# A two-layer fp32 encoder on one core: later casts of the turned attention weights, a new order of the output projections and end, and 16-bit DMA transposes for the residual and for rotated queries and keys

## The chip, the cores and the metric

The kernel runs on 1 core of one Trainium2 chip. The metric is the device time of one execution in microseconds; the kernel before was timed in 3 runs. Engines are named as in the profile: PE (TensorE matmul) and PEld (its weight load), DVE (VectorE), ACT (ScalarE), POOL (GpSimd), SP (SyncE, which issues almost all DMAs).

## The reference

An encoder trunk over 256 tokens of width 2048, all in float32: one even layer, one odd layer, a final RMSNorm.

```python
h = x
y = rms_norm(h, norm_g[0]); h = h + even_layer(y, w_in_even[0], w_out_even[0], rpb_b[0])
y = rms_norm(h, norm_g[1]); h = h + odd_layer(y, w_in_odd[0], w_out_odd[0], sinks_c[0], qnorm_d[0], knorm_d[0])
return rms_norm(h, final_g)
```

Each layer has 16 heads of 128 in two branches of 8 heads. Even: a dilated window attention with a distance penalty, and a two-dimensional neighbourhood attention with a learned bias. Odd: a windowed attention with a sink logit (branch C), and a dense attention with normalised and rotated queries and keys (branch D); four query heads share a key and value head. Each branch's output is multiplied by a SiLU gate; the gated outputs are concatenated and go through the output projection (2048 x 2048), whose result is added to h.

## The kernel before, in words

**The weight stream.** All projections are one stream of 272 weight tiles of 128 x 1024 floats, in the order of a list (`plan`). For each tile, called a weight step below and counted from 0: SP loads `wraw` (five buffers), ACT casts it to the rounded high part `whi` (L70), DVE subtracts to get the low part `wlo` (L71), both with three buffers, and PE runs its matmuls: high times high, high times low, low times high. The weights of a step are cast two steps ahead. In-projections of the even layer are steps 0 to 127, its output projection 128 to 159, in-projections of the odd layer 160 to 239, its output projection 240 to 271.

**Everything else runs beside it.** After each weight step, `step()` (L224) advances three queues of generators by one `yield`: `evac` (results out of PSUM), `post` (rotation of queries and keys), `bg` (attention, advanced twice if two are queued). What an engine does in which order follows from the order in which the program issues it and from a scheduler; DMAs issued with `pinned` (L86) keep their place in program order.

**Attention.** `attend` (L387) handles a pair of heads, in stages separated by yields: logits of both heads on PE, `probs` (exponentials on ACT, normalising at L430 or L432), `turned` and `joined`, `weigh` (the product with the values on PE). The probabilities must be transposed between `probs` and `weigh`. That is done in 16-bit halves: POOL takes the words apart (`ph`, L440), SP issues two DMA transposes (`pa`, L88), POOL joins the words again (`pt`, L451), ACT casts the high part (`pth`, L93), DVE subtracts for the low part (`ptl`, L94). `joined` issues the last three together, two yields after `turned`. Pairs 0 to 3 and 4 to 7 are the two branches of a layer; in the odd layer branch D (4 to 7) comes first.

**Rotation.** `normed_rope` (L329) scales queries or keys of branch D, rotates them on DVE into `ru`, and three yields later transposes them on PE (four 128 x 128 transposes, L353) into PSUM, from where ACT (L96) and DVE (L97) split them. It runs five times: one key pair, four query pairs.

**Output projection.** `close_layer` (L604) goes through the four column blocks of 512 (n) with all pairs but the last, then drains the attention queues, and then does the last pair's product for all four blocks in the tail. In the even layer the tail (L616) also makes the next layer's input: for each block, 8 transposes of h on PE (L626), splits into `x` by ACT and DVE, and the squares for the norm. In the odd layer the last pair's four weight tiles are brought in ahead, into the room of `x`, and `tail_odd` (L716) ends the kernel: for each half of the tokens (t) the last products, the squares, the reciprocal root by three Newton steps on DVE (L164), and the scaling of h and its way out in eight DMAs.

## Time and profile before

| | |
|---|---|
| time, median of 3 runs | 839.02 us (837.39 to 839.69) |
| profiled execution: its own time | 838.58 us |
| its span | 836.8 us, mean TensorE clock 0.993 |
| TensorE busy | 97% of the span |
| VectorE, ScalarE, GpSimd busy | 69%, 53%, 13% |
| chain that ended last | PE 72%, DMA 8%, DVE 7%, issue 4%, POOL 3%, ACT 3%, SPq 2% |
| read from HBM | 155.64 MB, 190 GB/s over the span |

The profile is of one execution. A row of the timeline gives start, duration, engine, line, operation, what it writes and reads, and in brackets how long the engine had been idle and what it waited for. Matmuls are pipelined, so the distance between their starts counts, not their duration. PEclk is the clock granted to TensorE as a share of full speed.

### The profile page before, as it was taken

Reading aid. Unit: us, or ns where it says so; the run is one execution under the profiler, and the core shown is the slowest. Engines: PE = TensorE matmul, PEld = TensorE weight load, DVE = VectorE, ACT = ScalarE, POOL = GpSimd, SP = SyncE. Lnnn points to the kernel's source line nnn. Section 1 sums busy time; section 2 is a strip of 40 time slices with the busy share of each in tenths; the row PEclk is TensorE's granted clock in tenths of the full one; section 3 lists DMA queues with packets and bytes.
Section 4 is the critical chain, followed back from the end, with each engine's and each line's share of the span. In section 5 each row is a group of like instructions: output and inputs, shape, how many; then the busy total and the mean of one; then the engine's idle time right before and its main releaser. Section 6 shows DMA issues by size and latency. Waiting matters only on the chain.

```text
span 836.8 us, 11845 instructions
## 1 busy us (share of the span) xinstructions
PE 813.5 (97%) x4344; PEld 695.9 (83%) x4344; DVE 576.5 (69%) x873; ACT 443.1 (53%) x706; POOL 108.6 (13%) x88
## 2 busy tenths in 40 slices
PE   7999999999999999999999999999999999998995
PEld 5888888888888888888888888888798888876884
DVE  5676775677756786687645877877966776675547
ACT  6755554554545554555443745667456655564433
POOL 0002020022203040040100000012222123211000
PEclk9999999999999999999999999999999999999998
DMA  8966775675755766675755555555676677867622
GB/s 276 375 221 210 264 189 202 210 212 156 223 200 153 248 179 217 199 193 186 213 184 194 168 185 185 192 168 173 176 185 195 201 237 196 210 198 207 209 88 100
DMA packets 90394, 166.91 MB, mean 199 GB/s; under 512 B 48928, under 2 KB 49824, under 8 KB 90272
## 3 DMA queue, kind: packets, MB, share of 16 engines
q1 hardware_dynamic: 90192, 166.14, 64.0%
q8 instruction: 34, 0.56, 0.3%
q14 instruction: 24, 0.20, 0.1%
q10 hardware_dynamic: 144, 0.02, 0.0%
HBM read 155.64 MB, written 3.05 MB: 190 GB/s over the span
## 4 chain that ended last, share of the span: by engine, by line
PE 72%; DMA 8%; DVE 7%; issue 4%; POOL 3%; ACT 3%; SPq 2%; POOLq 0%; DVEq 0%; ACTq 0%
PE ps_f L251 24%; PE ps_f L255 12%; PE ps_t L104 11%; PE ps_t L103 10%; PE ps_t L105 10%; DMA pa<-ph 4%; DVE wlo L71 3%; DMA wraw<-in_even_t 2%; SPq L88 2%; POOL ph L440 2%; POOL pt L451 2%; ACT whi L70 1%; DMA h<-in_x 1%; PE ps_out L104 1%; PE ps_out L105 1%
## 5 line engine op out<-in xcount | busy, mean ns | idle before, releaser
L71 DVE TENSOR_TENSOR wlo<-wraw,whi 128x1024 fp32r<-128x1024 f32 (+1 forms) x269 | 340.1, 1269 | 151.4 <-ACT whi L70 149.7
L70 ACT CAST whi<-wraw 128x1024 fp32r<-128x1024 f32 (+1 forms) x269 | 279.9, 1046 | 230.2 <-PE ps_t L105 120.6
L251 PE MATMUL ps_f<-x,whi 128*128 128x512 f32 x1184 | 373.0, 396 | 0.0
L255 PEld LDWEIGHTS ps_f<-x,wlo 128*128 128x128 f32 x1184 | 222.5, 189 | 58.0 <-DVE wlo L71 6.0
L255 PE MATMUL ps_f<-x,wlo 128*128 128x256 f32 x1184 | 234.3, 279 | 3.2 <-DVE wlo L71 3.0
L251 PEld LDWEIGHTS ps_f<-x,whi 128*128 128x128 f32 x1184 | 181.3, 189 | 0.4
L103 PE MATMUL ps_t<-whi,x 128*128 128x512 f32 (+1 forms) x256 | 98.0, 383 | 4.7 <-ACT x L96 4.7
L440 POOL COPY ph<-pr 128x1024 uint16<-128x1024 uint16 x32 | 40.3, 1261 | 443.9 <-ACT pr L430 264.1
L104 PE MATMUL ps_t<-wlo,x 128*128 128x512 f32 (+1 forms) x256 | 97.4, 381 | 0.3 <-DVE wlo L71 0.3
L104 PE MATMUL ps_t<-wlo,mh 128*128 128x512 f32 x240 | 95.1, 396 | 2.1 <-DVE wlo L71 2.1
L105 PE MATMUL ps_t<-whi,x 128*128 128x512 f32 (+1 forms) x256 | 97.1, 379 | 0.0
L103 PE MATMUL ps_t<-whi,mh 128*128 128x512 f32 x240 | 94.5, 394 | 2.0 <-ACT whi L70 2.0
L105 PE MATMUL ps_t<-whi,ml 128*128 128x512 f32 x240 | 94.1, 392 | 0.0
L93 ACT CAST pth<-pt 128x512 fp32r<-128x512 f32 x32 | 19.8, 620 | 84.9 <-POOL pt L451 84.9
L451 POOL COPY pt<-pa 128x1024 uint16<-128x1024 uint16 x32 | 54.2, 1693 | 45.3 <-DMA pa<-ph 45.3
L103 PEld LDWEIGHTS ps_t<-whi,x 128*128 128x128 f32 x256 | 48.7, 190 | 13.5 <-ACT x L96 5.3
L94 DVE TENSOR_TENSOR ptl<-pt,pth 128x512 fp32r<-128x512 f32 x32 | 22.1, 689 | 53.8 <-ACT pth L93 53.8
L105 PEld LDWEIGHTS ps_t<-whi,x 128*128 128x128 f32 x256 | 48.6, 190 | 9.1
L104 PEld LDWEIGHTS ps_t<-wlo,x 128*128 128x128 f32 x256 | 48.8, 191 | 8.9 <-DVE wlo L71 0.7
L104 PEld LDWEIGHTS ps_t<-wlo,mh 128*128 128x128 f32 x240 | 45.5, 190 | 12.4 <-DVE wlo L71 3.6
L103 PEld LDWEIGHTS ps_t<-whi,mh 128*128 128x128 f32 x240 | 45.5, 189 | 11.7 <-ACT whi L70 2.5
L105 PEld LDWEIGHTS ps_t<-whi,ml 128*128 128x128 f32 x240 | 45.5, 190 | 9.3
(116 smaller groups left out, 665.0 us busy)
## 6 DMA issues: line engine op xcount, KB each, us to landing
wraw<-in_even_f SPq DMA_DIRECT2D x96, 512.0 KB, 3.9
wraw<-in_odd_f SPq DMA_DIRECT2D x56, 512.0 KB, 4.0
wraw<-in_w_out_even SPq DMA_DIRECT2D x32, 512.0 KB, 3.3
wraw<-in_w_out_odd SPq DMA_DIRECT2D x32, 512.0 KB, 4.0
wraw<-in_even_t SPq DMA_DIRECT2D x31, 512.0 KB, 4.5
wraw<-in_odd_t SPq DMA_DIRECT2D x24, 512.0 KB, 3.3
h<-in_x SPq DMA_DIRECT2D x4, 512.0 KB, 8.1
bias<-in_bias_a SPq DMA_DIRECT2D x8, 256.0 KB, 5.5
```

What stands on the lines that cost most here:

```text
L70: nc.scalar.copy(self.hi[:, c], raw[:, c])
L71: nc.vector.tensor_sub(self.lo[:, c], raw[:, c], self.hi[:, c].bitcast(F32))
L88: tc.keep_in_program_order(nc.sync.dma_start(dst, src, **kw))
L93: nc.scalar.copy(hi, src)
L94: nc.vector.tensor_sub(lo, src, hi.bitcast(F32))
L103: nc.tensor.matmul(dst, lh, rh, start=first, stop=False, skip_group_check=True)
L104: nc.tensor.matmul(dst, lh, rl, start=False, stop=False, skip_group_check=True)
L105: nc.tensor.matmul(dst, ll, rh, start=False, stop=last, skip_group_check=True)
L251: nc.tensor.matmul(acc[:, f, :], w.hi[:, c], xx[k], start=k == 0, stop=False, skip_group_check=True)
L255: nc.tensor.matmul(acc[:, f, :S], w.lo[:, c], xh[k], start=False, stop=k == KC - 1, skip_group_check=True)
L440: nc.gpsimd.tensor_copy(halves, words)
L451: nc.gpsimd.tensor_copy(words.bitcast(U16).rearrange("p c (q s) -> p s c q", s=2), st[i])
```

## The change

- **Turning in two functions.** `turn` (POOL's halves, SP's two transposes) and `join` (POOL's words) are taken out of the attention, to be used in three places.
- **Attention.** `joined` comes one yield after the second `turned` instead of two; the cast of `pth` and the subtraction of `ptl` are a stage of their own, `parted`, a yield later. ACT's cast keeps its place in program order.
- **Queues.** `step()` advances `post` twice if two are queued. `need(pr)` advances the queues until a pair is done.
- **Rotation.** The four PE transposes become a turn: a yield, `turn`, two yields, `join`, a yield, then the split of the words, ACT's part of it in program order.
- **Residual.** For each finished column block `next_input` turns h in two parts (8 turns in all) and splits the words into `x`, where 32 PE transposes stood.
- **Output projection.** Two column blocks are accumulated side by side: six pairs of block 0, six of block 1, then pair 7 and pair 8 of the order for both; then blocks 2 and 3 one after the other with all eight pairs. Nothing waits for a drain before the last pair. In the odd layer the last four pairs of block 3 are kept for the end, their weights in the room of `x`; the squares of blocks 0 to 2 are taken as each is finished, and they are multiplied by the final gain ahead of the end.
- **End.** For each half of the tokens, the last four products of block 3, the square, and the reciprocal root as Sqrt on ACT, reciprocal and one Newton step on DVE; for the second half of the tokens the last product, its sum and square come in two parts of 256 columns. The output leaves in ten DMAs.

```diff
         for queue in (evac, post, bg):
             advance(queue)
+        if len(post) > 1:
+            advance(post)
...
+    def turn(tag, tag2, src, bufs):
+        halves = tp.tile([P, 2, 2, S], U16, tag=tag, name="halves", bufs=bufs)
+        across = tp.tile([P, 2, 2, S], U16, tag=tag2, name="across", bufs=bufs)
+        nc.gpsimd.tensor_copy(halves, src.bitcast(U16).rearrange("p t (k s) -> p t s k", s=2))
+        for t in range(2):
+            pinned(
+                across[:, :, :, t * P : (t + 1) * P].rearrange("p s c q -> p (s c) q"),
+                halves[:, t].rearrange("p s k -> p (s k)"), transpose=True,
+            )
+        return across
+
+    def join(tag, across, bufs):
+        words = tp.tile([P, 2, S], F32, tag=tag, name="words", bufs=bufs)
+        nc.gpsimd.tensor_copy(words.bitcast(U16).rearrange("p c (q s) -> p s c q", s=2), across)
+        return words
...
         nc.vector.tensor_add(u, u, w)
-        for _ in range(3):
-            yield
-        tr = ps_at.tile([P, 2, S], F32, tag="at", name="ps_tr")
-        for t in range(2):
-            for hh in range(2):
-                nc.tensor.transpose(tr[:, hh, t * P : (t + 1) * P], u[:, t, hh, :], ident)
+        yield
+        across = turn("tmp2", "tmp2", u.rearrange("p t h d -> p t (h d)"), 2)
+        yield
+        yield
+        words = join("tmp2", across, 2)
+        yield
         dst = pair(tag)
-        split(*dst, tr, scale)
+        tc.keep_in_program_order(nc.scalar.mul(dst[0], words, scale))
+        nc.vector.scalar_tensor_tensor(
+            out=dst[1], in0=words, scalar=scale, in1=dst[0].bitcast(F32), op0=ALU.mult, op1=ALU.subtract
+        )
...
+        def parted(i):
             hi = tp.tile([P, 2, S], F32R, tag="pth", name="pth")
             lo = tp.tile([P, 2, S], F32R, tag="ptl", name="ptl")
-            split(hi, lo, words)
+            tc.keep_in_program_order(nc.scalar.copy(hi, st[i]))
+            nc.vector.tensor_sub(lo, st[i], hi.bitcast(F32))
...
         turned(1)
         yield
-        yield
         joined(0)
         yield
         joined(1)
+        parted(0)
+        yield
+        parted(1)
         yield
...
+    def out_order(kind):
+        order = ORDER[kind]
+        seq = [(n, pr) for n in range(2) for pr in order[:6]]
+        seq += [(n, pr) for pr in order[6:] for n in range(2)] + [(2, pr) for pr in order]
+        return seq + [(3, pr) for pr in (order if kind == "even" else order[:4])]
...
-            for c in range(2):
-                tr = ps_at.tile([P, 2, S], F32, tag="at", name="ps_ht")
-                for i in range(2):
-                    for t in range(2):
-                        nc.tensor.transpose(
-                            tr[:, i, t * P : (t + 1) * P],
-                            h[n][:, t, (2 * c + i) * P : (2 * c + i + 1) * P], ident,
-                        )
+    def next_input(n):
+        across = [turn("lg", "pr", h[n][:, :, c * S : (c + 1) * S], 2) for c in range(2)]
+        for c in range(2):
+            words = join("lg", across[c], 2)
+            for i in range(2):
+                k = 4 * n + 2 * c + i
+                split(xh[k], xl[k], words[:, i, :], gcol[:, KC + k : KC + k + 1])
+        square_sums(parts1, n)
...
+    def scale_of(ss, rest):
+        root, y, x, half, u, r = [col(name) for name in ("root", "y", "x", "half", "u", "r")]
+        pin(nc.scalar.activation(root, ss, AF.Sqrt, bias=rest, scale=1.0 / D))
+        pin(nc.vector.tensor_scalar(x, ss, 1.0 / D, rest, ALU.mult, ALU.add))
+        pin(nc.vector.tensor_scalar_mul(half, x, -0.5))
+        pin(nc.vector.reciprocal(y, root))
+        pin(nc.vector.tensor_scalar(u, y, y, half, ALU.mult, ALU.mult))
+        pin(nc.vector.tensor_scalar(r, u, 1.5, y, ALU.add, ALU.mult))
+        return r
...
+    for j, pr in enumerate(late[:3]):
+        product_out(accs[1], final[j], pr, 1, False, False)
+    ss = []
+    for c in halves:
+        product_out(accs[1], final[3], late[3], 1, False, True, c)
+        ss.append(added(1, c))
+    rest = col("rest")
+    pin(nc.vector.tensor_scalar(rest, ss[0], 1.0 / D, sums[:, 1:2], ALU.mult, ALU.add))
+    r = scale_of(ss[1], rest)
+    finish(0, 1, r, halves[0])
+    finish(0, 1, r, halves[1])
+    finish(1, 1, r, scalar=True)
+    finish(3, 1, r, halves[0])
+    finish(3, 1, r, halves[1])
+    finish(2, 1, r)
```

What an engine has in its queue is compared at three places. First ACT at the last attention of branch C, where the output projection of the odd layer begins. In a row stand line, operation, what it writes and reads (numbers are tiles), and the shape; `pr` are the probabilities, L430 and, in the change, L443 normalise them. Before:

```order
L422 ACTIVATE pr_7389,den_7390<-lg_7336,mn_7335 128x257 x2
L70 CAST whi_7367<-wraw_7366 128x1024
L430 ACTIVATE pr_7389<-pr_7389,rden_7393 128x256 x2
L70 CAST whi_7398<-wraw_7397 128x1024
L93 CAST pth_7466<-pt_7464 128x512
L70 CAST whi_7429<-wraw_7428 128x1024
L93 CAST pth_7490<-pt_7488 128x512
```

And of the change the same stretch of ACT:

```order
L435 ACTIVATE pr_7400,den_7401<-lg_7347,mn_7346 128x257 x2
L443 ACTIVATE pr_7400<-pr_7400,rden_7404 128x256 x2
L70 CAST whi_7378<-wraw_7377 128x1024
L70 CAST whi_7410<-wraw_7409 128x1024
L70 CAST whi_7433<-wraw_7432 128x1024
L70 CAST whi_7453<-wraw_7452 128x1024
L457 CAST pth_7472<-words_7450 128x512
L70 CAST whi_7477<-wraw_7476 128x1024
L457 CAST pth_7494<-words_7470 128x512
```

Between the second head's normalising and the first `pth` there is one weight cast before, and four in the change.

Second, ACT in the output projection of the even layer, where column block 0 becomes the odd layer's input `x0`. Before, with `ps_ht` the PSUM tile that PE's transposes wrote:

```order
L185 ACTIVATE junk_4435,parts_3794<-h0_91 128x512
L185 ACTIVATE junk_4437,parts_3794<-h0_91 128x512
L96 ACTIVATE x0_87<-ps_ht_4417,gcol_95 128x256
L96 ACTIVATE x0_87<-ps_ht_4426,gcol_95 128x256
L96 ACTIVATE x0_87<-ps_ht_4417,gcol_95 128x256
L70 CAST whi_4484<-wraw_4483 128x1024
L96 ACTIVATE x0_87<-ps_ht_4426,gcol_95 128x256
```

And in the change, where `words` is POOL's joined tile and `whi_4246` and `whi_4264` are the weights of steps 147 and 148:

```order
L168 ACTIVATE junk_4176,parts_3794<-h0_91 128x512
L168 ACTIVATE junk_4178,parts_3794<-h0_91 128x512
L70 CAST whi_4228<-wraw_4227 128x1024
L168 ACTIVATE junk_4222,parts_3794<-h1_92 128x512
L168 ACTIVATE junk_4224,parts_3794<-h1_92 128x512
L70 CAST whi_4246<-wraw_4245 128x1024
L96 ACTIVATE x0_87<-words_4164,gcol_95 128x256 x2
L96 ACTIVATE x0_87<-words_4170,gcol_95 128x256 x2
L70 CAST whi_4264<-wraw_4263 128x1024
L70 CAST whi_4282<-wraw_4281 128x1024
L96 ACTIVATE x1_88<-words_4210,gcol_95 128x256 x2
```

The splits read POOL's tile instead of PE's, and stand two weight casts behind the block's squares, in front of the weight of step 148; the last product of block 0 is step 142.

Third, ACT at the first attention of branch D (probabilities `pr_5342` before). Before:

```order
L96 ACTIVATE qh_5284<-ps_tr_5279 128x512
L70 CAST whi_5316<-wraw_5315 128x1024
L422 ACTIVATE pr_5342,den_5343<-ps_s_5306,mn_5313 128x256 x2
L430 ACTIVATE pr_5342<-pr_5342,rden_5346 128x256 x2
L70 CAST whi_5351<-wraw_5350 128x1024
L422 ACTIVATE pr_5373,den_5374<-ps_s_5333,mn_5340 128x256 x2
L430 ACTIVATE pr_5373<-pr_5373,rden_5377 128x256 x2
L70 CAST whi_5387<-wraw_5386 128x1024
L93 CAST pth_5406<-pt_5404 128x512
```

And in the change, where `qh_5227` is the second pair of queries and `pr_5298` the first head's probabilities:

```order
L70 CAST whi_5307<-wraw_5306 128x1024
L304 ACTIVATE ge_5285<-qf_5281 128x512
L365 ACTIVATE qh_5227<-words_5203 128x512
L443 ACTIVATE pr_5298<-pr_5298,rden_5302 128x256 x2
L70 CAST whi_5343<-wraw_5342 128x1024
L435 ACTIVATE pr_5329,den_5330<-ps_s_5289,mn_5296 128x256 x2
L443 ACTIVATE pr_5329<-pr_5329,rden_5333 128x256 x2
L70 CAST whi_5369<-wraw_5368 128x1024
L457 CAST pth_5364<-words_5360 128x512
L70 CAST whi_5398<-wraw_5397 128x1024
```

The cast of the second queries now reads POOL's `words` and stands directly in front of the first head's normalising, where before it read PSUM and stood a weight cast ahead of the exponentials.

More of the change, by code (lines that the diff above doesn't have):

```diff
@@ L757, in encoder, with beside @@
-    close_layer(ORDER["odd"], tail_odd, ahead)
+    gfin, final = [], []
+    parts2 = sm.tile([P, 2, NN], F32, tag="parts", name="parts")
+    late = ORDER["odd"][4:]
+    def beside(n, i):
+        if (n, i) == (2, 0):
+            for m in range(NN):
+                gfin.append(pp.tile([P, 512], F32, tag="bias", name="gfin", bufs=4))
+                nc.sync.dma_start(gfin[m], a["final_g"][m * 512 : (m + 1) * 512].partition_broadcast(P))
+        if n == 2 and i % 2:
+            j = i // 2
+            room = X[j].rearrange("p k c t -> p (k c t)")
+            final.append(Weights(a["w_out_odd"][NN - 1][late[j]], room[:, :1024], room[:, 1024:]))
+        if (n, i) in ((2, 4), (2, 6), (3, 1)):
+            m = i // 2 - 2 if n == 2 else 2
+            for t in range(2):
+                nc.vector.tensor_mul(h[m][:, t, :], h[m][:, t, :], gfin[m])
@@ new lines, in encoder @@
+    accs = project_out("odd", lambda n: square_sums(parts2, n), beside)[NN - 1]
+    pin = tc.keep_in_program_order
+    full, halves = slice(0, 512), [slice(0, 256), slice(256, 512)]
+    sums = sm.tile([P, 2], F32, tag="sums", name="sums", bufs=1)
+    nc.vector.tensor_reduce(sums, parts2[:, :, : NN - 1], AX.X, ALU.add)
+    nc.vector.tensor_scalar(sums, sums, 1.0 / D, EPS, ALU.mult, ALU.add)
+    nc.scalar.activation(warm, sums[:, :1], AF.Sqrt)
+    col = lambda name: sm.tile([P, 1], F32, tag="rc_" + name, name="rc_" + name)
@@ new lines, in finish @@
+    def finish(n, t, r, cols=full, scalar=False):
+        y = h[n][:, t, cols]
+        if n == NN - 1:
+            pin(nc.vector.scalar_tensor_tensor(y, y, r, gfin[n][:, cols], ALU.mult, ALU.mult))
+        elif scalar:
+            pin(nc.scalar.mul(y, y, r))
+        else:
+            pin(nc.vector.tensor_scalar_mul(y, y, r))
+        pin(nc.sync.dma_start(out[t * P : (t + 1) * P, n * 512 + cols.start : n * 512 + cols.stop], y))
+    for j, pr in enumerate(late):
+        product_out(accs[0], final[j], pr, 0, False, j == 3)
```

146 lines of the change are left out of this document (42 added, 104 removed).

## The prediction

> **What bounds the kernel now.** I read the page's totals first, then the table of 20 us windows, and last the timeline around the places where TensorE loses time.
>
> ```profile
> PE 813.5 (97%) x4344; PEld 695.9 (83%) x4344; DVE 576.5 (69%) x873; ACT 443.1 (53%) x706; POOL 108.6 (13%) x88
> ```
>
> TensorE is busy 97% of the span, so only three things can shorten it: fewer matmuls, fewer stops of TensorE, a shorter end after the last matmul. In the windows below the columns are window, length, busy time (instructions) of PE, PEld, DVE, ACT and POOL, then TensorE's clock, DMA share, GB/s.
>
> ```profile
> 120.00:140.00 20.00, 19.54 (x98) 16.27 (x96) 14.28 (x16) 10.12 (x13) 0.00 (x0) 1.00 0.56 185
> 200.00:220.00 20.00, 19.19 (x111) 16.38 (x111) 15.75 (x22) 9.82 (x18) 8.85 (x6) 1.00 0.63 173
> ...
> 460.00:480.00 20.00, 20.00 (x101) 16.19 (x100) 16.36 (x25) 14.50 (x29) 0.00 (x0) 1.00 0.48 159
> 480.00:500.00 20.00, 20.00 (x95) 16.48 (x94) 14.92 (x32) 10.74 (x18) 0.00 (x0) 1.00 0.55 184
> 500.00:520.00 20.00, 20.00 (x92) 16.55 (x91) 14.53 (x32) 10.96 (x21) 0.00 (x0) 1.00 0.60 192
> ...
> 580.00:600.00 20.00, 20.00 (x119) 17.45 (x118) 19.10 (x42) 12.05 (x22) 5.88 (x4) 1.00 0.63 175
> 600.00:620.00 20.00, 18.23 (x118) 16.55 (x116) 16.59 (x27) 11.73 (x23) 2.50 (x3) 0.91 0.49 151
> ...
> 740.00:760.00 20.00, 18.77 (x85) 14.96 (x84) 12.65 (x21) 10.84 (x20) 4.36 (x4) 1.00 0.89 217
> 760.00:780.00 20.00, 17.19 (x74) 13.77 (x73) 12.44 (x13) 9.35 (x10) 0.94 (x1) 0.91 0.64 211
> ```
>
> A window loses its idle time plus (1 - clock) times 20 us. The even layer's two windows lose 0.46 + 0.81 = 1.27. The odd layer's dense attention (600:620) loses 1.77 + 1.80 = 3.57. The stretch where the windowed branch ends and the last projection begins (740 to 780) loses 1.23 + 2.81 + 1.80 = 5.84. The windows at 460 to 520, with 32 PE transposes in them, lose nothing. The last loss is of one kind, and the timeline of POOL, ACT and PE there shows it:
>
> ```profile
> 759.61 1.34 POOL L451 COPY pt<-pa 128x1024 uint16<-128x1024 uint16 x1 [5.61 <-DMA pa<-ph]
> ...
> 760.98 0.62 ACT L93 CAST pth<-pt 128x512 fp32r<-128x512 f32 x1 [5.38 <-POOL pt L451]
> 761.50 2.94 ACT L70 CAST whi<-wraw 128x1024 fp32r<-128x1024 f32 x3
> ...
> 759.93 0.39 PE L104 MATMUL ps_t<-wlo,mh 128*128 128x512 f32 x1
> 760.16 0.39 PE L105 MATMUL ps_t<-whi,ml 128*128 128x512 f32 x1
> 762.59 0.49 PE L103 MATMUL ps_t<-whi,mh 128*128 128x512 f32 x1 [2.05 <-ACT whi L70]
> 763.85 0.80 PE L104 MATMUL ps_t<-wlo,mh 128*128 128x512 f32 x1 [0.77 <-DVE wlo L71]
> 764.45 0.63 PE L105 MATMUL ps_t<-whi,ml 128*128 128x512 f32 x1
> 764.87 0.63 PE L103 MATMUL ps_t<-whi,mh 128*128 128x512 f32 x1
> ```
>
> ACT runs in order. Its cast of the turned probabilities (pth) stood 5.38 us waiting for POOL's copy, three weight casts (whi) queued behind it, PE ran out of weights for 2.05 and 0.77 us, and then ran matmuls 0.42 us apart instead of 0.23. So the cost of a turn is not its POOL or DMA time but whether ACT reaches its last cast too early.
>
> **Part by part.** First what a turn (POOL's halves, SP's two DMA transposes, POOL's words) and one weight step take, from the timeline at the first attention and from the page's groups:
>
> ```profile
> 70.98 1.04 POOL L440 COPY ph<-pr 128x1024 uint16<-128x1024 uint16 x1 [69.59 <-DVE pr L432]
> ...
> 72.05 2.61 SPq L88 DMA_TRANSPOSE pa<-ph  x2
> ...
> 76.02 1.51 POOL L451 COPY pt<-pa 128x1024 uint16<-128x1024 uint16 x1 [0.77 <-DMA pa<-ph]
> ```
> ```profile
> L71 DVE TENSOR_TENSOR wlo<-wraw,whi 128x1024 fp32r<-128x1024 f32 (+1 forms) x269 | 340.1, 1269 | 151.4 <-ACT whi L70 149.7
> L70 ACT CAST whi<-wraw 128x1024 fp32r<-128x1024 f32 (+1 forms) x269 | 279.9, 1046 | 230.2 <-PE ps_t L105 120.6
> ...
> L440 POOL COPY ph<-pr 128x1024 uint16<-128x1024 uint16 x32 | 40.3, 1261 | 443.9 <-ACT pr L430 264.1
> ...
> L451 POOL COPY pt<-pa 128x1024 uint16<-128x1024 uint16 x32 | 54.2, 1693 | 45.3 <-DMA pa<-ph 45.3
> ```
>
> From 70.98 to 77.53 a turn takes 6.55 us undisturbed; a second one right behind it ends 2.6 later, since SP issues its pair in 2.61. A weight step is 12 matmuls 0.227 apart, 2.72 us. Three buffers of whi let the cast of step k start when PE ends step k-3; cast and wlo end 2.6 us later (0.24 + 1.05 + 1.27), and PE wants them 5.67 us later, so a weight has 3.1 us of slack. What ACT waits beyond that stops PE.
>
> *Later casts of pth.* By the order, the distance on ACT from normalising to pth grows by three weight casts in the even layer (8.2 us, more than the 5.38 waited) and by two to three in the windowed branch. I take the even loss as gone, -1.27, and of the 5.84 all but 0.4: -5.4. Bounds: none of it (the waits only move) to -1.3 and -5.8.
>
> *No PE transposes.* All 52 go (32 at L626, 20 at L353).
>
> ```profile
> 482.87 0.82 PE L626 MATMUL ps_ht<-ident,h 128*128 128x128 f32 x6
> 483.44 0.48 PE L104 MATMUL ps_t<-wlo,x 128*128 128x512 f32 x1
> ```
>
> Six of them and the step to the next matmul take 0.57 us, 0.095 each: 52 x 0.095 = -4.9, all on PE and so all on the path.
>
> *Residual turns.* Eight more turns, whose words ACT splits (L96) in its queue among the weight casts.
>
> ```profile
> pa<-ph SPq DMA_TRANSPOSE x64, 2.6
> ...
> L96 ACT ACTIVATE x<-ps_ht,gcol 128x256 fp32r<-128x256 f32 x16 | 6.9, 467 | 0.5 <-DVE x L97 0.5
> ```
>
> The last product of column block 0 is weight 142 (the 15th of the projection). From its end: two adds 1.5 with the way out of PE, halves 1.3, SP's second transpose issued 1.3 later and landed 2.6 after that, words 1.7: the first words are there at 8.4, the second, one pair of transposes later, at 10.9. ACT's order has the four splits between the casts of weights 147 and 148. So ACT is through them at 10.9 + 2 x 0.47 = 11.8, the cast of 148 ends at 12.9 and its wlo at 14.2. PE comes to weight 148 after five steps, at 13.6, and to its low part at 13.85: a stop of about 0.4. Blocks 2 and 3 stand the same six weights apart, block 1 looser. Three stops of 0.4 if nothing else is in the way, a little more where DVE or POOL is: +2.0. Bounds: 0 (the windows at 460 to 520 lose nothing today) and 8 (four stops like the 2.05 above). SP's weight loads stand behind eight pairs of 2.6 us, but five raw buffers are 13.6 us of work.
>
> *Rope turns.* Five more turns. The normalising of a head's probabilities is this row:
>
> ```profile
> 749.46 0.91 ACT L430 ACTIVATE pr<-pr,rden 128x256 f32<-128x256 f32 x2
> ```
>
> Before, a rotated query reached its split over four PE transposes; now over 6.55 us. ACT's cast qh of the second query (L365) waits for its words, and by the order the normalising of the first dense head's probabilities, its turn and its pth stand behind it. From the sum ru on: add 0.7 (wlo takes 1.27 for twice the width), turn 6.55, cast 0.62, its two normalisings 0.91, turn 6.55, cast 0.62: 15.9 us. PE has, from the low part of the weight that DVE issues just before that add, four steps, six 256-wide matmuls (half of 0.227 each) and two matmuls left, 10.9 + 0.7 + 0.4 = 12.0. Timed from the same wlo, PE would stop 15.9 - 12.0 = 3.9 if that wlo came just in time, and 2 if it came 2 us early; I take 3. A stop like this brings the 1.80 of half clock seen in 600:620. The later heads have the same knot (qh of the third query stands before pth of the second head): 3.3 with their clock loss. In all 8.1 where 3.57 stood: +4.5. Bounds: 0 (both stops as long as now) to 11 (three stops of the kind of 760:780, 4.61 each, less 3.57).
>
> *The end.* The timeline of PE, DVE and ACT there:
>
> ```profile
> 826.38 0.39 PE L105 MATMUL ps_t<-x,ml 128*128 128x512 f32 x1
> ...
> 827.19 0.68 DVE L511 TENSOR_TENSOR h<-ps_t,h 128x512 f32<-128x512 f32 x1
> ...
> 827.96 0.63 ACT L738 ACTIVATE junk<-h 128x512 bf16<-128x512 f32 x1 [0.40 <-DVE fhead L745]
> ...
> 828.72 0.21 DVE L168 TENSOR_SCALAR rc_x<-fss,fhead 128x1 f32<-128x1 f32 x1
> ...
> 830.34 0.27 DVE L176 TENSOR_SCALAR rc_t<-rc_z,rc_half 128x1 f32<-128x1 f32 x1
> 830.64 0.21 DVE L178 TENSOR_SCALAR fr<-rc_t,rc_z 128x1 f32<-128x1 f32 x1
> 830.89 2.74 DVE L723 SCALAR_TENSOR_TENSOR h<-h,fr,gfin 128x512 f32<-128x512 f32 x4
> ```
>
> The span ends at 836.8, so 10 us lie behind the last matmul (826.77). The add and the square work on half the width: -0.5 of 1.3. The root took 828.72 to 830.85, 2.13; a Sqrt on ACT, a reciprocal and one of the three Newton pairs (0.55) remain, about 1.2: -0.9. Sqrt is not in this trace: between 0.2 (the small column operations above) and all of the 0.9. Of the four scalings (2.74) ACT takes one: -0.5, of which two more output DMAs give part back. I take -1.6, bounds -2.4 and 0.
>
> Premultiplying by the gain and the squares beside the last projection lie under the 7 us that DVE, and the 9 that ACT, have free in each of the windows from 740 to 780: nothing, as long as PE's weights come first there; if they don't, the slack of 3.1 us a step is drawn on and little more.
>
> **Sum.** -1.3 - 5.4 - 4.9 + 2.0 + 4.5 - 1.6 = -6.7 us. The profiled execution took 838.6 us (span 836.8 and 1.8 around it), 0.4 under the median of 839.0: 831.9 for the one, **832.3** for the other.
>
> **Rivals.** *Full gain.* The new waits fit in the slack, as the transposes of today do in 460:520, whose windows show 20.00 busy. Then the +6.5 goes: 825.8. Against it: ACT's casts in front of the weights are in the order.
>
> *No net gain.* The turns stop PE as the branch end does today (residual 8, rope 11 instead of 2.0 and 4.5): 832.3 + 12.5 = 844.8; with half of that 838.6. The half is likelier than the whole, since a wait under the slack of 3.1 us stops nothing.
>
> *Slower: DVE behind POOL.* The two engines hold each other up:
>
> ```profile
> 746.45 1.04 POOL L440 COPY ph<-pr 128x1024 uint16<-128x1024 uint16 x1 [12.37 <-ACT pr L430]
> ...
> 746.54 2.02 DVE L71 TENSOR_TENSOR wlo<-wraw,whi 128x1024 fp32r<-128x1024 f32 x1
> ```
>
> The wlo that met a POOL copy took 2.02 instead of 1.27, ending 1.07 after the copy did. In 580 to 620 DVE is busy 35.7 of 40 us, so 4.3 are free, and five rope turns bring 5 x 2.95 (1.26 + 1.69) = 14.8 us of POOL copies to about that place. If all meet DVE, it is 10.5 us over. That replaces my 4.5 by 10.5 and two more windows at 0.91 (3.6): 832.3 + 9.6 = 841.9. At 460 to 520 DVE is busy 45.8 of 60 us against 23.6 us of new copies; if three quarters of these meet it, 3.5 more: 845.4. I take 844. It decides from the point where 4.3 of the 14.8, 29%, fall on a DVE operation; but DVE waits today for ACT and PE in between, and that the copies fall on the densest part is half the cases at most. The Trainium skill, page "SBUF — State Buffer", section "Who interferes with whom", has it as a rule: a DVE instruction with two SBUF inputs and a GpSimd instruction that reads SBUF exclude each other for the whole instruction, whoever starts first. By that rule, the trace agrees: 2.02 is the rest of the copy (0.95) and 1.07 more.
>
> *It does not do what it says*, the casts moving without the waits going: their -6.7 is not had, and 839.0 is left; the order speaks against it.
>
> **How the numbers follow.** A measurement of this kernel can tell about 0.3%, 2.5 us, from no change. Forecast 0.42 (829 to 836.4), full gain 0.22 (about 826), no net gain 0.16 (about 838.6, of it 0.04 below 836.5 and 0.02 above 841.5), slower by DVE and POOL 0.16 (about 844), not as it says 0.04 (same). Faster 0.42 + 0.22 + 0.04 = 0.68; same 0.10 + 0.04 = 0.14; slower 0.16 + 0.02 = 0.18. The range takes in the forecast's bounds and most of the full gain below and the weaker half of the slower cases above: 824.5 to 842.5.
>
> **What would show it.** Right: no PE transposes; 26 more turning copies on POOL beside the 64 of L440 and L451; clock 1.00 at the branch end and PE not waiting for whi there; new waits of PE for whi or wlo at the residual (460 to 520) and at the first two dense heads (about 570 to 610), 2 and 8 us with the clock's part; 8.4 us from the last matmul to the end. Wrong: 460 to 620 as full as today (full gain), wlo far over 1.27 on average there (the slower rival), or the branch end still stopping.

## The result, and the profile after

The changed kernel took 842.56 us (median of 5 runs, 841.95 to 843.32), the kernel before 837.39 us beside it (5 runs, 834.62 to 839.69). The ratio is 1.0062, 95% interval 1.0036 to 1.0089: slower by 0.6%, where a gain of 0.8% was forecast. The range ended at 842.5, and 0.18 had been given to slower.

The profiled execution took 842.56 us with a span of 840.8, 4.0 longer than before. The page's totals of the changed kernel:

```profile
PE 809.7 (96%) x4298; PEld 692.9 (82%) x4298; DVE 587.2 (70%) x854; ACT 448.8 (53%) x712; POOL 152.9 (18%) x114
```

TensorE is busy 3.8 us less and GpSimd 44 us more. What TensorE waited for in all, the longest wait last in each row:

```profile
PE ps_out L103 <- ACT pth L457: 11.4, 5, 4.6
PE ps_t L103 <- ACT x L96: 5.2, 2, 5.0
PE ps_t L104 <- DVE wlo L71: 4.6, 6, 1.3
PE ps_t L103 <- DVE h L744: 1.3, 2, 0.8
PE ps_f L246 <- DVE wlo L71: 0.5, 1, 0.5
```

The first row is most of the story: the weighing (ps_out) waits for the cast of the turned probabilities. Before, the only wait of the weighing was this one:

```profile
PE ps_out L104 <- DVE ptl L94: 0.3, 1, 0.3
```

In the changed kernel's list the second row is the start of the kernel, as before. The windows of the changed kernel that answer to those shown of before:

```profile
120.00:140.00 20.00, 20.00 (x103) 17.01 (x102) 13.43 (x15) 9.47 (x12) 0.16 (x1) 1.00 0.58 193
200.00:220.00 20.00, 20.00 (x118) 17.51 (x118) 18.33 (x25) 11.05 (x20) 10.26 (x6) 1.00 0.63 204
...
440.00:460.00 20.00, 17.93 (x77) 14.01 (x76) 14.31 (x17) 11.83 (x18) 8.39 (x6) 1.00 0.77 241
460.00:480.00 20.00, 19.36 (x86) 15.72 (x85) 12.66 (x14) 9.13 (x12) 3.45 (x3) 1.00 0.68 217
480.00:500.00 20.00, 19.43 (x88) 15.80 (x87) 16.41 (x29) 9.97 (x15) 5.73 (x4) 1.00 0.67 208
...
540.00:560.00 20.00, 18.92 (x94) 15.30 (x93) 17.07 (x32) 10.39 (x20) 6.06 (x4) 1.00 0.58 182
560.00:580.00 20.00, 15.42 (x72) 13.18 (x73) 10.20 (x13) 11.04 (x23) 5.60 (x4) 0.91 0.59 160
580.00:600.00 20.00, 18.61 (x108) 16.05 (x106) 17.15 (x42) 12.22 (x30) 7.05 (x5) 1.00 0.66 173
600.00:620.00 20.00, 18.12 (x102) 16.23 (x103) 17.18 (x29) 11.58 (x22) 6.35 (x4) 0.91 0.44 146
620.00:640.00 20.00, 16.79 (x123) 16.25 (x122) 11.85 (x17) 9.86 (x19) 4.82 (x4) 0.91 0.64 176
...
740.00:760.00 20.00, 19.67 (x98) 16.23 (x97) 14.25 (x24) 12.30 (x22) 6.48 (x6) 1.00 0.61 191
760.00:780.00 20.00, 20.00 (x96) 16.76 (x95) 10.77 (x11) 8.71 (x10) 1.36 (x1) 1.00 0.74 231
```

The even layer's two windows are full now and the branch end (740 to 780) all but 0.3 us, as forecast. The residual (440 to 500) loses 3.3. The dense heads (540 to 640) lose 12.1 of idle time and three times 1.8 of clock. The kernel before lost 2.3 of idle time and once 1.8 there; beside the window of 600 to 620 it was idle only in these two:

```profile
560.00:580.00 20.00, 19.86 (x107) 16.92 (x106) 12.68 (x24) 14.09 (x39) 5.58 (x4) 1.00 0.65 188
620.00:640.00 20.00, 19.66 (x137) 18.09 (x136) 13.12 (x17) 10.88 (x21) 4.68 (x3) 1.00 0.73 194
```

The same by stages: the start of a stage is the first matmul of the same weight in both traces, so that each stage holds the same work.

| stage | before | after | difference |
|---|---|---|---|
| start to the even output projection | 385.85 | 384.62 | -1.2 |
| even output projection, residual, first odd weights (to 524.17, 523.11) | 138.32 | 138.49 | +0.2 |
| dense heads (to the start of weight 208 at 628.54, 640.67) | 104.37 | 117.56 | +13.2 |
| windowed branch (to 727.92, 738.49) | 99.38 | 97.82 | -1.6 |
| odd output projection, to the last matmul (826.38, 832.51) | 98.46 | 94.02 | -4.4 |
| behind the start of the last matmul | 10.42 | 8.27 | -2.1 |

The first stage and those from the windowed branch on went about as forecast. The residual's stage gave nothing where about 1 us had been forecast (3.0 of transposes less 2.0 of waits), and the dense heads took more than all the others gave. How a dense head stops TensorE, in the timeline of ACT, POOL and PE at the first one:

```profile
555.46 0.63 ACT L365 ACTIVATE qh<-words 128x512 fp32r<-128x512 f32 x1 [2.30 <-POOL words L325]
555.99 0.90 ACT L443 ACTIVATE pr<-pr,rden 128x256 f32<-128x256 f32 x2
...
563.91 0.62 ACT L457 CAST pth<-words 128x512 fp32r<-128x512 f32 x1 [2.47 <-POOL words L325]
...
553.99 1.44 POOL L325 COPY words<-across 128x1024 uint16<-128x1024 uint16 x1 [3.90 <-DMA across<-halves]
556.95 1.36 POOL L314 COPY halves<-pr 128x1024 uint16<-128x1024 uint16 x1 [1.53 <-ACT pr L443]
...
562.20 1.67 POOL L325 COPY words<-across 128x1024 uint16<-128x1024 uint16 x1 [0.59 <-DMA across<-halves]
...
564.58 0.38 PE L103 MATMUL ps_out<-pth,vh 128*128 128x256 f32 x1 [4.63 <-ACT pth L457]
564.80 0.45 PE L105 MATMUL ps_t<-whi,x 128*128 128x512 f32 x1
565.05 0.63 PE L103 MATMUL ps_t<-whi,x 128*128 128x512 f32 x1
565.48 0.63 PE L104 MATMUL ps_t<-wlo,x 128*128 128x512 f32 x1
```

It is the chain that the prediction described: words of the rope turn, ACT's qh, normalising, halves, transposes, words, pth. TensorE stood at the weighing for 4.63 us and then ran at half rate (0.43 between starts). At the second head the words of the probabilities had long been there:

```profile
585.79 1.36 POOL L325 COPY words<-across 128x1024 uint16<-128x1024 uint16 x1 [2.33 <-DMA across<-halves]
...
599.33 1.32 POOL L325 COPY words<-across 128x1024 uint16<-128x1024 uint16 x1 [3.87 <-DMA across<-halves]
...
600.69 0.63 ACT L365 ACTIVATE qh<-words 128x512 fp32r<-128x512 f32 x1 [2.28 <-POOL words L325]
601.22 1.12 ACT L457 CAST pth<-words 128x512 fp32r<-128x512 f32 x2
...
601.88 0.39 PE L103 MATMUL ps_out<-pth,vh 128*128 128x256 f32 x1 [3.27 <-ACT pth L457]
```

The words were ready at 587.15, and pth was cast at 601.22, because in ACT's queue it stood behind the qh of the next pair of queries, which waited for its own rope turn until 600.65.

### The profile page after: what moved, and what is told of

It is laid out like the page before. It is cut to its first block, busy times and chain, and to the rows that moved or that the text cites. A ratio compares the mean times of both kernels' runs of the same rounds, so it can differ in the third digit from the quotient of the medians.

```text
span 840.8 us, 11823 instructions
## 1 busy us (share of the span) xinstructions
PE 809.7 (96%) x4298; PEld 692.9 (82%) x4298; DVE 587.2 (70%) x854; ACT 448.8 (53%) x712; POOL 152.9 (18%) x114
## 4 chain that ended last, share of the span: by engine, by line
PE 78%; DVE 7%; DMA 5%; POOL 3%; ACT 2%; issue 2%; SPq 2%; POOLq 0%; DVEq 0%; ACTq 0%
PE ps_f L242 28%; PE ps_f L246 14%; PE ps_t L104 10%; PE ps_t L105 10%; PE ps_t L103 10%; DMA across<-halves 3%; SPq L88 2%; DVE wlo L71 2%; POOL halves L314 2%; POOL words L325 1%; DMA wraw<-in_even_t 1%; ACT whi L70 1%; PE ps_out L103 1%; PE ps_out L104 1%; PE ps_out L105 1%
## 5 line engine op out<-in xcount | busy, mean ns | idle before, releaser
L71 DVE TENSOR_TENSOR wlo<-wraw,whi 128x1024 fp32r<-128x1024 f32 (+1 forms) x269 | 347.1, 1292 | 168.5 <-ACT whi L70 167.4
L325 POOL COPY words<-across 128x1024 uint16<-128x1024 uint16 x45 | 73.0, 1622 | 79.1 <-DMA across<-halves 79.1
L314 POOL COPY halves<-pr 128x1024 uint16<-128x1024 uint16 x32 | 41.0, 1281 | 254.8 <-DVE pr L445 159.0
L104 PEld LDWEIGHTS ps_t<-wlo,x 128*128 128x128 f32 x256 | 49.4, 193 | 11.7 <-DVE wlo L71 3.5
L397 POOL TENSOR_TENSOR bias<-maskB,rpb 128x512 f32<-128x512 f32 x8 | 12.5, 1568 | 140.0 <-DMA rpb<-rows 140.0
L435 ACT ACTIVATE pr<-lg,mn 128x256 f32<-128x256 f32 (+1 forms) x48 | 24.0, 501 | 16.3 <-POOL halves L314 15.2
```

Of the source, the lines that this page charges most:

```text
L71: nc.vector.tensor_sub(self.lo[:, c], raw[:, c], self.hi[:, c].bitcast(F32))
L104: nc.tensor.matmul(dst, lh, rl, start=False, stop=False, skip_group_check=True)
L314: nc.gpsimd.tensor_copy(halves, src.bitcast(U16).rearrange("p t (k s) -> p t s k", s=2))
L325: nc.gpsimd.tensor_copy(words.bitcast(U16).rearrange("p c (q s) -> p s c q", s=2), across)
L397: nc.gpsimd.tensor_tensor(b, maskB.unsqueeze(1).to_broadcast([P, 2, S]), raw, op=ALU.subtract)
L435: nc.scalar.activation(p[:, t, :W], lg[:, t, :W], AF.Exp, bias=mn[:, t : t + 1], scale=-1.0, accum_out=den[:, t : t + 1],)
```

## The experiments

Two theories were tried first. **W**: the chain through ACT (qh, normalising, turn, pth) is what is long. **C**: the rival of the prediction, VectorE held up by GpSimd's copies. Two more came later, when W fell short. **S**: the second advance of `post` in each step starts the dense heads too early for a chain that takes as long as ever; and against it **T**: only the length and load of the turns count. Times are medians of 4 to 10 runs. Ratios are to the kernel before on the same chip; e1 to e4, e5 to e8, e9 to e12 and e13 to e15 ran on four different chips, so a difference between two of these groups is good to about 2 us. "Dense and windowed" is the length of those two stages by the traces (before 203.8, changed kernel 215.4). The traced executions of e9 and e6 took 832.72 and 836.28 us, 3.1 and 2.0 above their medians.

| run | us | ratio, 95% interval | dense and windowed |
|---|---|---|---|
| e1: rope on TensorE | 833.95 | 0.9956 (0.9934 to 0.9979) | 206.7 |
| e2: residual on TensorE | 842.68 | 1.0054 (1.0035 to 1.0073) | 216.2 |
| e3: both on TensorE | 832.90 | 0.9935 (0.9915 to 0.9955) | 206.5 |
| e4: e1 and dummy rope turns | 842.80 | 1.0056 (1.0034 to 1.0078) | 215.1 |
| e5: changed kernel, later weighing | 843.73 | 1.0089 (1.0064 to 1.0114) | 217.8 |
| e6: changed kernel, post once | 834.33 | 0.9972 (0.9954 to 0.9991) | 207.8 |
| e7: e3, later weighing | 835.09 | 0.9981 (0.9966 to 0.9995) | 208.5 |
| e8: e2, later weighing | 841.99 | 1.0062 (1.0034 to 1.0089) | 216.0 |
| e9: e3, post once | 829.63 | 0.9906 (0.9875 to 0.9936) | 203.7 |
| e10: changed kernel, heads queued later | 837.12 | 0.9992 (0.9975 to 1.0008) | 210.7 |
| e11: kernel before, post twice | 841.16 | 1.0048 (1.0031 to 1.0064) | 206.6 |
| e12: kernel before, rope turns | 837.41 | 0.9994 (0.9982 to 1.0006) | 205.2 |
| e13: e14 and dummy rope turns | 832.51 | 0.9960 (0.9945 to 0.9974) | 204.2 |
| e14: e1, post once | 830.61 | 0.9937 (0.9920 to 0.9953) | 202.5 |
| e15: e2, post once | 835.30 | 0.9986 (0.9973 to 0.9999) | 209.2 |

**e1, rope on TensorE.** The lines of the kernel before in `normed_rope`:

```diff
-        yield
-        across = turn("tmp2", "tmp2", u.rearrange("p t h d -> p t (h d)"), 2)
-        yield
-        yield
-        words = join("tmp2", across, 2)
-        yield
+        for _ in range(3):
+            yield
+        tr = ps_at.tile([P, 2, S], F32, tag="at", name="ps_tr")
+        for t in range(2):
+            for hh in range(2):
+                nc.tensor.transpose(tr[:, hh, t * P : (t + 1) * P], u[:, t, hh, :], ident)
         dst = pair(tag)
-        tc.keep_in_program_order(nc.scalar.mul(dst[0], words, scale))
...
+        split(*dst, tr, scale)
```

> The changed kernel with the rotated queries and keys transposed on TensorE as before (20 transposes, no rope turn); residual turns and all else stay. Theory W (ACT's cast qh waits for the words of the rope turn, the dense heads' normalising, turn and pth queue behind it, TensorE reaches the weighing first): the four stops at pth (11.4 us in all) and their half clock go, 20 transposes cost 1.9 again: 842.6 - 13 = 829 to 831. Theory C (VectorE and GpSimd hold each other up, five turns of 2.95 us of copies): also faster, by about 10, 832. This run alone does not tell them apart; the next dummy run does.

833.95: 8.6 us of the loss go with the rope turns, less than W's 12 to 14. The dense heads still stop TensorE.

**e2, residual on TensorE.** The 32 transposes of the kernel before in `next_input`:

```diff
-        across = [turn("lg", "pr", h[n][:, :, c * S : (c + 1) * S], 2) for c in range(2)]
         for c in range(2):
-            words = join("lg", across[c], 2)
+            tr = ps_at.tile([P, 2, S], F32, tag="at", name="ps_ht")
+            for i in range(2):
+                for t in range(2):
+                    nc.tensor.transpose(
+                        tr[:, i, t * P : (t + 1) * P],
+                        h[n][:, t, (2 * c + i) * P : (2 * c + i + 1) * P], ident,
+                    )
...
-                split(xh[k], xl[k], words[:, i, :], gcol[:, KC + k : KC + k + 1])
+                split(xh[k], xl[k], tr[:, i, :], gcol[:, KC + k : KC + k + 1])
```

> The changed kernel with the residual rows transposed on TensorE as before (32 transposes, no residual turn); rope turns stay. In the changed kernel TensorE waits for wlo 0.70, 1.30, 0.64 and 0.56 us between 440 and 500 us. If these come from the residual turns they go, and 32 x 0.095 = 3.0 us of transposes come back: 842 (841 to 843), no measurable difference. If the later loss at the dense heads had begun here (a late start of the odd layer), it would shrink too: 835 or less.

842.68 against 842.56, as expected: the residual's turns cost about what its transposes cost on TensorE (3.2 us of waits for wlo, by the stops listed above, against 3.0). The dense heads are no better for it (216.2).

**e3, both.** The edits of e1 and e2 together.

> The changed kernel with both put back on TensorE, so that only the later casts, the side-by-side columns, the double advance of post and the new end remain. Theory W: as the run with rope on TensorE, 829 to 831. By the landmarks of the two traces (even layer -1.5, branch C and last projection -6.0, end -2.1 against the kernel before), 837.4 - 9.6 = 828 if the dense heads stay as in the kernel before.

832.90, some 2 to 4 us more than W said. What is left in the dense heads shows in TensorE's waits of this run, whose list begins:

```profile
PE ps_t L103 <- ACT x L96: 5.8, 3, 4.8
PE ps_out L103 <- ACT pth L454: 4.5, 4, 1.6
PE ps_tr L363 <- DVE ru L357: 1.6, 2, 1.4
```

With no rope turn in the program, TensorE still waits 4.5 us for pth. So a turn of the probabilities can be late without any help from rope, and W isn't the whole.

**e4, dummy turns.** e1, and between its yields a whole turn of `ru` whose words nobody reads (in a buffer that is idle in the odd layer):

```diff
+        halves = tp.tile([P, 2, 2, S], U16, tag="rpb", name="halves", bufs=1)
+        across = tp.tile([P, 2, 2, S], U16, tag="tmp2", name="across", bufs=2)
+        src = u.rearrange("p t h d -> p t (h d)")
+        nc.gpsimd.tensor_copy(halves, src.bitcast(U16).rearrange("p t (k s) -> p t s k", s=2))
+        for t in range(2):
+            pinned(
+                across[:, :, :, t * P : (t + 1) * P].rearrange("p s c q -> p (s c) q"),
+                halves[:, t].rearrange("p s k -> p (s k)"), transpose=True,
+            )
...
+        join("rpb", across, 1)
```

> As the run with rope on TensorE, and besides each rope turn is still made in full (halves, two DMA transposes, words) at the same places, only nobody reads its words; the result is not affected. Theory W: nothing waits for them, so within 1.5 us of the run with rope on TensorE, 829 to 832. Theory C: the copies hold VectorE up as in the changed kernel, so most of the 13 us stays: 838 to 843.

842.80, 8.9 above e1: here C had it right. How ten copies cost that much is seen at the second query pair. POOL, DVE and PE of e4:

```profile
543.41 1.35 POOL L325 COPY words<-across 128x1024 uint16<-128x1024 uint16 x1 [4.32 <-DMA across<-halves]
...
543.56 1.16 DVE L161 SCALAR_TENSOR_TENSOR drr<-rs_t,rs_z 128x4 f32<-128x4 f32 x1
...
548.42 0.68 DVE L357 TENSOR_TENSOR ru<-ru,rw 128x512 f32<-128x512 f32 x1
...
549.16 0.66 PE L374 MATMUL ps_tr<-ident,ru 128*128 128x128 f32 x4 [1.72 <-DVE ru L357]
```

And the same instructions in e1, whose queues have the same order:

```profile
541.99 0.16 DVE L161 SCALAR_TENSOR_TENSOR drr<-rs_t,rs_z 128x4 f32<-128x4 f32 x1
...
545.86 0.68 DVE L357 TENSOR_TENSOR ru<-ru,rw 128x512 f32<-128x512 f32 x1
...
546.60 0.66 PE L363 MATMUL ps_tr<-ident,ru 128*128 128x128 f32 x4
```

An operation of four numbers per row takes 0.16 us in e1; in e4 it met GpSimd's copy and took 1.16, ending with the copy (544.72 and 544.76). VectorE is packed there, so ru came late and TensorE waited 1.72 for it where it had waited for nothing. In all, e4 waits 3.3 us more than e1 for ru and 2.5 more for pth, and loses 3.4 us to half clock where e1 loses none.

So C is real. How far it carries over to the changed kernel is less clear. The waits for ru belong to the transposes on TensorE, which the changed kernel doesn't have; its stops at the dense heads are at pth, but for one of 1.01 us for wlo. Yet its VectorE was held up by the same copies, at the same place:

```profile
541.80 1.25 DVE L161 SCALAR_TENSOR_TENSOR drr<-rs_t,rs_z 128x4 f32<-128x4 f32 x1
```

This is the end of the reciprocal root of the second pair of queries, at the head of the chain to the first pth. Summed over all operations that took at least 0.1 us more than the median of their kind, VectorE was held up between 520 and 640 for 8.5 us in e4, 4.5 in e1, 6.1 in the changed kernel and 4.8 in the kernel before.

**e5, later weighing.** Three yields more between the last pth and `weigh` in the dense branch:

```diff
         parted(1)
         yield
+        if shared and bias is None:
+            for _ in range(3):
+                yield
```

> The changed kernel as it is, rope and residual turns and all their copies, only that in the dense branch three more yields stand between the last pth and the weighing. The dummy run left 5 us of doubt: there too TensorE stopped at pth. Theory W (TensorE comes to the weighing before the chain qh, normalising, turn, pth is through; nothing is slow as such): the stops at pth (11.4 us) go and with them the half clock of three windows (3 x 1.8): 826 to 830. Theory C (GpSimd's copies hold VectorE up): the copies are all still there, 837 or more.

843.73, no gain. But the run didn't make what it was meant to make. In TensorE's queue the weighing of the first pair of heads moved from weight 188 to 189 only, that of the second stayed at 198, the third moved from 204 to 205 and the fourth from 213 to 216: the scheduler places instructions by its own reckoning, and a yield later in the program isn't a step later in the queue. TensorE's waits at pth did fall from 11.4 to 6.4 us, but 3.2 of waits for wlo at other places came up, and the time didn't fall. It doesn't tell the theories apart.

**e6, post once.**

```diff
-        if len(post) > 1:
-            advance(post)
```

> The changed kernel without the second advance of the post queue, so that rotation and the start of each dense head move a yield later per step, as in the kernel before. Theory W: it matters where the heads start against the rope turns, so the stops at pth change, 830 to 836 if it was the double advance that brought the weighing forward, 842 if not. Theory C: the same copies at other places, 840 to 844.

834.33: two lines, and 8.2 us are back with every turn in place. That is what C could not give. In TensorE's queue the first pair's weighing goes from weight 188 to 192, and TensorE's waits at pth fall from 11.4 to 3.1:

```profile
PE ps_t L103 <- ACT x L96: 5.0, 1, 5.0
PE ps_t L104 <- DVE wlo L71: 3.6, 5, 1.3
PE ps_out L104 <- DVE ptl L456: 3.4, 3, 2.7
PE ps_out L103 <- ACT pth L455: 3.1, 5, 1.5
```

**e7 and e8, later weighing in e3 and e2.** The edit of e5 with two and three yields.

> Both transposes on TensorE as in the third run, and two more yields before the dense branch's weighing. There TensorE still waited 4.5 us for pth. Theory W: those go, 832.9 - 4.5 = 828 to 829. Theory C says nothing to gain here: 833.

> Residual on TensorE, rope turns as in the change, three more yields before the weighing. Theory W: as the late weighing with residual turns, since the residual's turns (3.2 us of stops) cost what its transposes (3.0) cost: 826 to 830, and up to 1.9 below both on TensorE with late weighing, whose 20 rope transposes it lacks. Theory C: 837 or more.

835.09 and 841.99: misses, for the reason seen at e5 (in e7 the first pair's weighing stayed at weight 188). Together with e6 they led to theory S: not when the weighing is issued but when the head's whole attention starts.

**e9, e3 with post once.** The edits of e3 and e6.

> Both transposes on TensorE, and post advanced once per step: of the change only the later casts, the column order and the end are left. By the order the dense heads' weighing stands at weights 190, 200, 206, 216 again, as before the change, where the double advance has it at 188, 196, 204, 212. Theory S (the second advance of post starts the dense heads two to four weight steps early, and TensorE then waits at pth for a chain that takes as long as ever): the 4.5 us of pth stops left in the third run shrink, 832.9 - 3 = 829 to 831. Theory T (only the turns' own length and load count): 833, no difference.

829.63, as S says, and the lowest median of all: 0.9906 of the kernel before, 13 us below the changed kernel. Of TensorE's waits at pth 0.4 is left; its list, without the wait at the start of the kernel, begins:

```profile
PE ps_out L104 <- DVE ptl L453: 1.5, 4, 0.5
PE ps_t L103 <- DVE h L744: 1.3, 2, 0.8
PE ps_bc L184 <- DVE rb L183: 0.8, 1, 0.8
PE ps_out L103 <- ACT pth L452: 0.4, 1, 0.4
```

**e10, heads queued later.** The changed kernel with

```diff
     def when_ready(i, st, s):
+        for _ in range(3):
+            yield
```

> The changed kernel with rope and residual turns and the double advance, but each dense head is queued three yields later; by the order its weighing stands at weights 190, 198, 206, 216 instead of 188, 198, 204, 213. Theory S: the first and last two heads no longer stop TensorE, the second (unmoved) does: 834 to 838. Theory T: 842.

837.12, within S's span.

**e11, kernel before with post twice.** The two lines that e6 takes out, put into the kernel before.

> The kernel before with nothing but the second advance of post. By the order the dense heads' weighing moves from weights 190, 200, 206, 216 to 188, 196, 204, 212. Theory S: stops at pth as in the third run (4.5 us), of which what the kernel before loses there is saved: 837.4 + 2 to + 4 = 839.5 to 841.5. Theory T: no turn is added, 837.4.

841.16, 4.0 slower without any turn added, as S says. New waits at pth of 3.3 us; the list begins:

```profile
PE ps_t L103 <- ACT x L96: 5.4, 2, 5.1
PE ps_out L103 <- ACT pth L93: 3.3, 4, 1.6
PE ps_tr L355 <- DVE ru L349: 2.4, 2, 2.2
```

**e12, kernel before with rope turns.** `turn`, `join` and the changed `normed_rope` put into the kernel before, post once.

> The kernel before with nothing but the rope turns in place of the 20 transposes on TensorE; post is advanced once. By the order the weighing moves two weight steps back (192, 202, 209, 217). Theory S: the turns alone cost what they add on POOL and VectorE and a part of the chain, at most 4, and 1.9 come back: 836 to 840. Theory T: most of the 13 us of the change's dense region is there: 847 or more.

837.41 against 837.19 beside it: no difference. Alone, the five turns give back what they save in transposes.

**e13 and e14, the dummy turns again.** e4 and e1 with post once.

> Rope on TensorE with the dummy rope turns beside it (nobody reads their words), residual turns, post advanced once. Load alone (theory C): 8.8 us above the next run, as between the dummy run and its pair with the double advance. Early start (theory S): the heads are back at weights 190, 200, 206, 216, the slack is there, 1 to 4 us above the next run.

> The same without the dummy turns: rope on TensorE, residual turns, post advanced once. By the residual turns' 1.0 us (first against third run): 829.6 + 1.0 = 830.6 under either theory.

832.51 and 830.61: the same ten copies that cost 8.9 us with the early heads cost 1.9 with the heads at their old places. VectorE was held up for over 8 us in both (by the sum used at e4), so the hold-up alone doesn't set the price.

**e15, rope turns with residual on TensorE, post once.** The edits of e2 and e6.

> Residual on TensorE, rope turns, post advanced once. With the double advance the rope turns cost 842.7 - 832.9 = 9.8 us. If their cost does not depend on the advance: 829.6 + 9.8 = 839. Theory S: 834.3 less the 0.1 to 1 of the residual turns, 833.3 to 834.2, so the rope turns cost about 4 there.

835.30: one us above what S said, and 5.7 above e9, where with the double advance the rope turns cost 9.8. By the traces the heads' weighing stands at weights 192, 202, 209 and 217 here, later than in the kernel before, and the loss is in the windowed branch (105.6 us long against 99.4 before), not in the dense heads (103.6 against 104.4); e6 has the same (104.6 and 103.2).

## Why the prediction was wrong

Step by step, the change is now: casts, columns and end -7.8 (e9 against the kernel before, 829.6 to 837.4); the second advance of `post` +3.3 (e3 against e9); residual turns +1.0 (e1 against e3); rope turns +8.6 (the changed kernel against e1). That makes 842.5. By the ratios, which take the chip out, the four are -7.9, +2.4, +1.8 and +8.9. The prediction had -8.3 for the first, nothing for the second, -1.0 for the third and +2.6 for the fourth, each with its share of the transposes. So two steps failed: the size of the rope turns, and the advance of `post`, which had no term. They don't simply add up, as the runs with all four combinations show:

| rope transposed | post once | post twice |
|---|---|---|
| on TensorE, residual turns | 830.61 (e14) | 833.95 (e1) |
| by turns, residual turns | 834.33 (e6) | 842.56 (changed kernel) |
| on TensorE, residual on TensorE | 829.63 (e9) | 832.90 (e3) |
| by turns, residual on TensorE | 835.30 (e15) | 842.68 (e2) |

- *Later casts* (-1.3 and -5.4): right as far as the stages tell. The even layer gave 1.2, the windowed branch and the last projection 6.0, and the clock at the branch end is 1.00. No run takes the casts without the new order of the columns.
- *No PE transposes* (-4.9): the time came off TensorE, but 3.2 of it came back as waits for wlo at the residual, and the 1.9 of rope many times over.
- *Residual turns* (+2.0): a little low. Four stops of 0.70, 1.30, 0.64 and 0.56, 3.2 us, at weights 148, 150, 157 and 165. Three are where the prediction had them; the longest is at the block that it called looser.
- *The end* (-1.6): -2.1 behind the last matmul, but TensorE now waits 1.3 for VectorE's sum (ps_t <- h, L744): 0.8 before the second half of the tokens and 0.5 before its last product's second part. The sum didn't have that wait; net -0.8.
- *Rope turns* (+4.5, bounds 0 to 11): here it failed. The turns alone cost 8.6 us net of the 1.9 of transposes saved (against e1) or 9.8 (e2 against e3), so 10.5 to 11.7 where the sum had 4.5. That is at the upper bound, whose own working, three stops of 4.61 less 3.57, gives 10.3 and not 11. The chain of the first head was right (3 us of stop forecast, 4.63 measured), and so was the half clock. Too small was "3.3 with their clock loss" for the later heads: 3.27, 2.31 and 0.90 at pth, each of the first two followed by a window at 0.91. The account closes: against e1 the changed kernel waits 6.7 us more at pth and loses 5.1 to half clock, and it is spared 1.9 of transposes and 1.6 of waits for ru; that makes 8.3 of the 8.6.
- *The step that was left out*: the second advance of `post` had no term at all. It stood in the diff, and TensorE's queue has the dense heads' weighing at weights 188, 198, 204 and 213 where it was 190, 200, 206 and 216. For the first head the prediction took TensorE's way to the weighing from the new order, and so had the early start in its 3 us without naming it; for the later heads it had not. Without any turn added, these two lines cost 4.0 (e11); with the turns in place, taking them out gives 8.2 back (e6). And the rope turns cost 4 to 5 us more with post advanced twice than with post advanced once (the columns of the table).
- *The rivals*. "No net gain" had the rope turns at 11, about what they measured, but with 8 for the residual instead of the 3.2 measured, and no advance. The one on the slower side had nearly the time (844), which is in good part luck. That VectorE and GpSimd hold each other up was shown by e4, with operations of 0.16 us stretched to 1.16 and more, and the changed kernel has such operations too. But the price hangs on the slack: 8.9 us (e4) or 1.9 (e13) for the same copies. And in the changed kernel VectorE was held up only 1.2 us more than before (6.08 against 4.84), which speaks against this rival as the main cause without ruling it out as a part. The Trainium skill, page "SBUF — State Buffer", section "Who interferes with whom", has it that a VectorE instruction with two SBUF inputs and a GpSimd instruction that reads SBUF exclude each other for the whole instruction. The trace of e4 agrees: the operation took 1.16 us and ended with the copy.

Open: how the 8.6 us of the rope turns in the changed kernel divide between ACT's qh standing in front of pth and the load of the copies, which also delays the query that qh waits for. No run takes away the one and keeps the other.

## What to carry to other kernels

A transpose that moves off a full engine isn't paid for by its own time but by what it holds up: the instructions that stand behind its result, and those that meet its copies, even when nobody reads the result (e4). Here the same five turns cost nothing in the kernel before (e12), 4 to 6 us after the other changes (e6 against e14, e15 against e9; 3 to 7 by the ratios), and 9 to 10 with the heads started early (the changed kernel against e1, e2 against e3). When a queue of stages is advanced faster, price each stage that starts earlier against the chains it still has to wait for. And a yield more in the program is not a step later on the engine when a scheduler has the last word; look at the order before trusting such an experiment.

## What the runs showed of the hardware

A VectorE operation on 4 numbers per row waited for the rest of a GpSimd copy: 1.16 us instead of 0.16. It was not the only one: five such operations took 1.01 to 1.26 us between 520 and 640 in e4, and five took 1.01 to 1.25 in the changed kernel. So a chain of dependent small operations, such as a reciprocal root, paid about 1 us for each copy that it met in this way. VectorE operations that read PSUM were not held up: in the changed kernel 25 began while a copy ran, and none took longer than usual by more than 0.01 us.

TensorE's half clock came in pieces of 3.4 us, or 6.8, and not after every stop of a given length: it followed stops of 1.77 us (kernel before) and 1.62 (e15), but not those of 2.21 (e11) and 2.24 (e4).
